# Up projection of a gated MLP: the sums of weight quarters made by VectorE in place of GpSimd

## The chip, the cores and the metric

The kernel runs on one core of one Trainium2 chip. The metric is the device time of one launch in microseconds, and several runs are given by their median. The engines are named as in the profile: PE is TensorE, DVE is VectorE, ACT is ScalarE, POOL is GpSimd, SP is SyncE, whose queue issues most of the transfers.

## The reference, cut to what matters

One layer of an encoder: a Fourier mixer, then a gated MLP with a centred convolution over positions. The change lies in the MLP's first matrix product.

```
D_MODEL = 1024; SEQ = 1024; D_FF = 2816; CONV_WIDTH = 3      # float32

def conv_gated_ffn(h, w_up, conv_w, conv_b, w_down):
    u = h @ w_up                                             # (1024, 1024) @ (1024, 5632)
    up = jnp.pad(u, ((0, 0), (1, 1), (0, 0)))
    u = up[:, :-2] * conv_w[0] + up[:, 1:-1] * conv_w[1] + up[:, 2:] * conv_w[2] + conv_b
    val, gate = u[..., :D_FF], u[..., D_FF:]
    return (jax.nn.gelu(gate, approximate=False) * val) @ w_down

# in the layer:
    h = modulate(x, sh2, sc2)
    y = conv_gated_ffn(h, ...)
    x = layer_norm(ALPHA * x + g2 * y, ...)
```

## The kernel before, in words

**Precision.** Every large product is made of three matmuls of a reduced-precision type: an operand is split into a high half (a copy by ScalarE, line 52) and a low half (source minus high half, by VectorE, line 53), and `hl3` (lines 292 to 294) adds high x high, high x low and low x high. A matmul that uses a weight's low half is the third of each three, line 294.

**Up projection.** The 2,816 columns of value and of gate are cut in 22 blocks of 128 each (`j`, 0 to 21). Blocks 0 and 1 are computed plainly (`first_mm`). From block 2 on, each block is one step of a scheme with seven products in place of eight: the two raw weight tiles of a block (`wu`, 512 KB each, loaded by `up_load`) hold four quarters A11, A21 (first tile) and A12, A22 (second tile), each [128, 4, 128]. Lines 764 to 767 make four sums of them: S1 = A21 + A22, S2 = S1 - A11, S3 = A11 - A21, S4 = A12 - S2. S1 and S2 share the tile in slot 31, S3 and S4 that in slot 32, so the sums of the next block can be written only when the last readers in this block are done.

The seven weight operands of a block, in the order of the products 0 to 6, are A11, S2, A12, S1, S3, S4, A22. `a_split` splits each into a_0 to a_6. The right-hand operands are quarters of the modulated, transposed activations (`h2t`, halves `Hh` and `Hl`) and the combinations T1, T2, T3, T4 of them, made once, in block 2. A product is 12 matmuls of 128x512 (four chunks of the inner dimension by three), a block 84. The results are added up by ScalarE (`p`) and VectorE (`u`, `uv`, `ug`), then convolved (line 678 on ScalarE, 679 and 680 on VectorE), put through GELU (685), multiplied (688 to 690) and written to DRAM by a transfer that GpSimd issues (691).

**Block 2** also finishes the plain blocks 0 and 1, makes T1 and T2 (line 658), adds to quarters in place with eight accumulating transfers that GpSimd issues (line 739), and splits T1 to T4. It runs by an order that is written out by hand for PE, DVE and ACT (`manual_schedule`, the table `between`); GpSimd and SP, and all engines from block 3 on, are put in order by the framework's scheduler. `A_first` gives the buffers of a_n in blocks 2 to 4: a_4 of block 2 lies in slot 30, into which the second raw tile of block 3 is loaded later.

**Down projection.** Seven passes over the block products, with the same scheme; it reads the blocks back from DRAM.

Of the kernel before, what the change touches and what calls it, by code (L numbers as in the profile page):

```python
# [11 lines left out]
ALU = mybir.AluOpType  # L12
# [23 lines left out]
def encoder_layer(ctx: ExitStack, tc: tile.TileContext, I, out: bass.AP):  # L36
    nc = tc.nc
    act, dve, pool, pe, sp = nc.scalar, nc.vector, nc.gpsimd, nc.tensor, nc.sync
# [6 lines left out]
    def slot(i, shape, dt, name):  # L45
        return big.tile([128] + list(shape), dt, tag=f"s{i}", name=name)
# [4 lines left out]
    def split(hi, lo, src, eng=None):  # L51
        act.activation(hi, src, AF.Copy)  # L52
        (eng or dve).tensor_tensor(lo, src, hi, ALU.subtract)  # L53

    def E(name):
        return pool if name in ON_POOL else dve
# [37 lines left out]
    def bank(i, name, shape=(512,)):  # L94
        return ps.tile([128] + list(shape), F32, tag=f"b{i}", name=name)
# [3 lines left out]
    def xbank(name):  # L99
        n_x[0] += 1  # L100
        return bank(n_x[0] % 8, name)
# [189 lines left out]
    def hl3(ps_ap, hi_l, lo_l, hi_r, lo_r, first, last):  # L291
        pe.matmul(ps_ap, hi_l, hi_r, start=first, stop=False)  # L292
        pe.matmul(ps_ap, hi_l, lo_r, start=False, stop=False)  # L293
        pe.matmul(ps_ap, lo_l, hi_r, start=False, stop=last)  # L294
# [252 lines left out]
    def up_load(j):  # L547
        sl = {0: (24, 27), 1: (40, 41), 3: (0, 30)}.get(j, (27, 30) if j % 2 else (28, 29))
        raws[j] = []
        for q in range(2):  # L550
            r = slot(sl[q], [4, 256], F32, f"wu{j}_{q}")
            sp.dma_start(r, I["w_up"][j, q])
            raws[j].append(r)
# [87 lines left out]
    def t_op(name, n, pieces):  # L641
        hi, lo = [], []
        for i in range(2):
            h = slot(T_slots[16 + 4 * n + 2 * i], [2, 512], F32R, f"T{name}h{i}")
            l = slot(T_slots[17 + 4 * n + 2 * i], [2, 512], F32R, f"T{name}l{i}")
            for q in range(2):
                split(h[:, q, :], l[:, q, :], pieces[2 * i + q])
                hi.append(h[:, q, :])
                lo.append(l[:, q, :])
        ops[name] = (hi, lo)  # L650

    def comb(name, x, y, op, sl):
        out_ = []
        for i in range(2):
            v = slot(sl + i, [2, 512], F32, f"{name}_{i}") if sl is not None else None
            for q in range(2):
                o = x[2 * i + q] if v is None else v[:, q, :]
                E(name).tensor_tensor(o, x[2 * i + q], y[2 * i + q], op)
                out_.append(o)
        return out_  # L660
# [4 lines left out]
    def plain_mm(acc, w, v, g):  # L665
        for k in range(KT):
            hl3(acc, *w[k, v], g(Hh[k]), g(Hl[k]), k == 0, k == KT - 1)

    def gated(j, u_v, u_g):
        gate_out(j, u_g, gate_conv(j, u_v, u_g))  # L670

    def gate_conv(j, u_v, u_g, tts=None, vs=(0, 1)):
        tv = []
        for v in vs:
            u = (u_v, u_g)[v]
            tt = slot(tts[v] if tts else 3 + (2 * j + v) % 3, [S], F32, f"t{j}_{v}")
            w = cw[:, j, v, :]
            act.activation(tt, u, AF.Identity, scale=w[:, 1:2], bias=w[:, 3:4])  # L678
            dve.scalar_tensor_tensor(tt[:, 1:S], u[:, 0 : S - 1], w[:, 0:1], tt[:, 1:S], ALU.mult, ALU.add)  # L679
            dve.scalar_tensor_tensor(tt[:, 0 : S - 1], u[:, 1:S], w[:, 2:3], tt[:, 0 : S - 1], ALU.mult, ALU.add)  # L680
            tv.append(tt)
        return tv

    def gate_out(j, u_g, tv):
        act.activation(tv[1], tv[1], AF.Gelu)
        gg = u_g

        dve.scalar_tensor_tensor(gg[:, 0:512], tv[0][:, 0:512], -1.0, tv[1][:, 0:512], ALU.mult, ALU.mult)
        dve.tensor_tensor(gg[:, 512:513], tv[0][:, 512:513], tv[1][:, 512:513], ALU.mult)
        dve.tensor_tensor(gg[:, 513:1024][:, ::-1], tv[0][:, 513:1024], tv[1][:, 513:1024], ALU.mult)  # L690
        pool.dma_start(gd[j], gg)  # L691
# [6 lines left out]
    def first_mm(j, gi):  # L698
        g = GRP[gi]
        for v in range(2):  # L700
            dst = g(uf[j][v])
            acc = bank((4, 5, 0, 1, 3)[n_f1[0] % 5], f"x{j}_{gi}{v}", tuple(dst.shape[1:]))
            n_f1[0] += 1
            plain_mm(acc, first_w[j], v, g)
            act.activation(dst, acc, AF.Copy)
# [23 lines left out]
    def t3_split(qs):  # L729
        for q in qs:  # L730
            split(ops["T3"][0][q], ops["T3"][1][q], B[0, 1][q])

    def minus(x):
        for v in x:
            act.activation(v, v, AF.Copy, scale=-1.0)

    def add_to(x, y):
        for q in range(4):
            pool.dma_start(x[q], y[q], accum_op=ALU.add)
# [4 lines left out]
        1: (lambda: t3_split(range(4)), lambda: tt.extend(gate_conv(0, *uf[0], tts=(34, 4), vs=(1,)))),  # L744
        2: (None, lambda: t_op("T4", 2, T2)),
        3: (None, lambda: gate_out(0, uf[0][1], tt)),
# [9 lines left out]
    for j in range(2, NB):  # L756
        up_load(j)
        raw = raws[j]
        A11, A21 = raw[0][:, :, 0:128], raw[0][:, :, 128:256]
        A12, A22 = raw[1][:, :, 0:128], raw[1][:, :, 128:256]  # L760
        S12 = slot(31, [2, 4, 128], F32, f"S12_{j}")
        S34 = slot(32, [2, 4, 128], F32, f"S34_{j}")
        S1, S2, S3, S4 = S12[:, 0], S12[:, 1], S34[:, 0], S34[:, 1]
        pool.tensor_tensor(S1, A21, A22, ALU.add)  # L764
        pool.tensor_tensor(S2, S1, A11, ALU.subtract)
        pool.tensor_tensor(S3, A11, A21, ALU.subtract)  # L766
        pool.tensor_tensor(S4, A12, S2, ALU.subtract)  # L767

        a_of = (A11, S2, A12, S1, S3, S4, A22)
        o_of = []  # L770

        def a_split(upto):
            while len(o_of) < min(upto, 7):
                n = len(o_of)
                o = slot(A_first.get(j, A_slots)[n], [2, 4, 128], F32R, f"a{j}_{n}")
                split(o[:, 0], o[:, 1], a_of[n])
                o_of.append(o)

        def product(n, tname):
            a_split(n + 1)  # L780
            acc = xbank(f"x{j}_{n}")
            th, tl = ops[tname]
            for kt in range(4):
                hl3(acc, o_of[n][:, 0, kt, :], o_of[n][:, 1, kt, :], th[kt], tl[kt], kt == 0, kt == 3)
            if j == 2:
                first, then = between[n]
                if first:
                    first()
                a_split(n + 4)
                if then:  # L790
                    then()
            return acc

        if j == 2:

            T1 = comb("T1", B[0, 1], B[0, 0], ALU.subtract, 25)
            minus(B[0, 1])
            add_to(B[0, 1], B[1, 1])
            T2 = comb("T2", B[1, 1], T1, ALU.subtract, 46)
            t_op("T2", 1, T2)  # L800
            minus(B[1, 0])
            add_to(T2, B[1, 0])
            a_split(1)
            first_mm(0, 3)
            tt = gate_conv(0, *uf[0], tts=(34, 4), vs=(0,))
            a_split(3)
            first_mm(1, 3)
        if j == NB - 1:
            g2 = slot(29, [D], F32, "g2")
            row_bcast(G2, g2, xbank)  # L810
        p12 = slot(6, [2, 512], F32, f"p12_{j}")
        u34 = slot(7, [2, 512], F32, f"u34_{j}")
        p1, u2, u3, u4 = p12[:, 0], p12[:, 1], u34[:, 0], u34[:, 1]
        uv_ = slot((2 * j) % 3, [S], F32, f"uv{j}")
        ug_ = slot((2 * j + 1) % 3, [S], F32, f"ug{j}")
        x = product(0, "B11")
        act.activation(p1, x, AF.Copy)
        x = product(1, "T2")
        dve.tensor_tensor(u2, x, p1, ALU.add)
        x = product(2, "B21")  # L820
        dve.tensor_tensor(uv_[:, 0:512], x, p1, ALU.add)
        x5 = product(3, "T1")
        dve.tensor_tensor(u4, x5, u2, ALU.add)
        x = product(4, "T3")
        dve.tensor_tensor(u3, x, u2, ALU.add)
        dve.tensor_tensor(ug_[:, 512:], x5, u3, ALU.add)
        x = product(5, "B22")
        dve.tensor_tensor(uv_[:, 512:], x, u4, ALU.add)
        x = product(6, "T4")
        dve.tensor_tensor(ug_[:, 0:512], u3, x, ALU.subtract)  # L830
        if j == 2:
            front.close()
        gated(j, uv_, ug_)
# [423 lines left out]
```

## Time and profile before

| | |
|---|---|
| median of 3 runs | 838.65 us (838.61 to 841.0) |
| the profiled execution | 838.94 us |
| its span, first to last instruction | 837.0 us |
| mean granted clock of TensorE | 0.987 of full speed |
| PE busy | 791.4 us (95%) |
| DVE busy | 691.4 us (83%) |
| ACT busy | 399.3 us (48%) |
| POOL busy | 253.5 us (30%) |

Times within a trace are microseconds from the span's start. In a timeline a row is a start, a duration and the instruction; a bracket at its end is the time for which the engine sat idle before it, and what released it. Durations of instructions that follow each other overlap by some 0.07 us on DVE and 0.16 us on PE, so the step from start to start is what a further instruction adds. The up projection by blocks of seven products runs from 218 to 608 us, the down projection behind it.

### The profile page before, as it was taken

To read this page: it belongs to the slowest core of one execution; us is meant where nothing else is said; L and a number is where in the kernel's file an instruction comes from. 1 tells how busy PE (TensorE), PEld (TensorE's weight loads), DVE (VectorE), ACT (ScalarE), POOL (GpSimd) and SP (SyncE) were. 2 spreads that over 40 slices of the span, in tenths; PEclk is the share of its full clock that TensorE was granted. 3 is DMA by queue.
4 is the path that set the end of the run, shared out by engine and by line. 5 is a ranking of instruction groups with operands and counts; after the bars stand their busy time and mean duration, and the time that the engine had idled before them with its cause. 6 is when DMAs were issued, how large, how long until landed. Compare 5 with 4: busy or idle time off the path is not lost.

```text
span 837.0 us, 10967 instructions
## 1 busy us (share of the span) xinstructions
PE 791.4 (95%) x4039; PEld 644.0 (77%) x4039; DVE 691.4 (83%) x1002; ACT 399.3 (48%) x605; POOL 253.5 (30%) x214
## 2 busy tenths in 40 slices
PE   2899999999989999999999999999999999999991
PEld 1566677899868888888888888888888878887881
DVE  6958866865899999998888888888688794557997
ACT  7643625785654534444444444344454425335611
POOL 2163004321743353343433333331000112602303
PEclk9999999999999999999999999999999999999996
DMA  9977864533731413222222222210498897998903
GB/s 340 376 261 251 277 225 170 201 114 141 138 113 51 151 53 114 102 86 76 76 79 98 94 83 90 88 51 25 152 369 324 257 327 141 190 163 213 302 14 126
DMA packets 51702, 136.01 MB, mean 162 GB/s; under 512 B 5672, under 2 KB 6824, under 8 KB 51648
## 3 DMA queue, kind: packets, MB, share of 16 engines
q1 hardware_dynamic: 39872, 105.16, 35.5%
q0 software_dynamic: 11776, 30.15, 15.2%
q8 instruction: 31, 0.51, 0.2%
q14 instruction: 23, 0.19, 0.1%
HBM read 110.39 MB, written 19.92 MB: 156 GB/s over the span
## 4 chain that ended last, share of the span: by engine, by line
PE 78%; DVE 11%; DMA 4%; ACT 3%; issue 3%; POOL 1%; POOLq 0%; SPq 0%; DVEq 0%; ACTq 0%
PE x L294 16%; PE x L292 16%; PE x L293 16%; PE o L293 7%; PE o L294 7%; PE o L292 7%; PE ada L139 2%; DMA gA<-gd 1%; DMA aw<-in_ada_w_dram 1%; DMA xr<-in_xm_dram 1%; DVE t L679 1%; DVE wa L366 1%; DVE we L366 1%; PE trm L530 1%; DVE sta L234 1%
## 5 line engine op out<-in xcount | busy, mean ns | idle before, releaser
L292 PE MATMUL x<-Hh,a 128*128 128x512 f32 (+2 forms) x448 | 161.7, 361 | 1.4 <-ACT a L52 1.4
L293 PE MATMUL x<-Hl,a 128*128 128x512 f32 (+2 forms) x448 | 161.0, 359 | 0.9 <-DVE Hl L53 0.9
L294 PE MATMUL x<-Hh,a 128*128 128x512 f32 (+2 forms) x448 | 160.9, 359 | 0.6 <-DVE a L53 0.6
L293 PE MATMUL o<-d_1l,d_0h 128*128 128x512 f32 (+1 forms) x299 | 113.8, 382 | 0.4 <-DVE d_1l L53 0.4
L294 PE MATMUL o<-d_1h,d_0l 128*128 128x512 f32 (+1 forms) x299 | 113.1, 381 | 0.0
L292 PE MATMUL o<-d_1h,d_0h 128*128 128x512 f32 (+1 forms) x299 | 102.1, 382 | 0.6 <-ACT d_0h L52 0.6
L52 ACT ACTIVATE a<-S 128x512 fp32r<-128x512 f32 x80 | 49.5, 628 | 101.6 <-PE x L294 75.6
L292 PEld LDWEIGHTS x<-Hh,a 128*128 128x128 f32 x448 | 84.6, 189 | 14.5 <-ACT a L52 1.8
L294 PEld LDWEIGHTS x<-Hh,a 128*128 128x128 f32 x448 | 84.5, 189 | 13.7 <-DVE a L53 1.1
L293 PEld LDWEIGHTS x<-Hl,a 128*128 128x128 f32 x448 | 84.5, 189 | 13.6 <-DVE Hl L53 1.1
L53 DVE TENSOR_TENSOR a<-S,a 128x512 fp32r<-128x512 f32 x80 | 65.2, 816 | 0.7
L292 PEld LDWEIGHTS o<-d_1h,d_0h 128*128 128x128 f32 x299 | 56.0, 188 | 12.0 <-ACT d_0h L52 1.0
L293 PEld LDWEIGHTS o<-d_1l,d_0h 128*128 128x128 f32 x299 | 56.1, 188 | 11.9 <-DVE d_1l L53 1.1
L294 PEld LDWEIGHTS o<-d_1h,d_0l 128*128 128x128 f32 x299 | 56.2, 188 | 10.7
L691 POOL DMA_DIRECT2D gd<-ug x20 | 11.5, 573 | 170.0 <-DVE ug L690 170.0
L53 DVE TENSOR_TENSOR a<-wu,a 128x512 fp32r<-128x512 f32 x60 | 53.5, 892 | 1.3 <-ACT a L52 1.1
L52 ACT ACTIVATE a<-wu 128x512 fp32r<-128x512 f32 x60 | 37.3, 625 | 19.0 <-PE x L294 12.1
L53 DVE TENSOR_TENSOR d_1l<-wd,d_1h 128x1024 fp32r<-128x1024 f32 (+1 forms) x37 | 43.9, 1190 | 2.8 <-ACT d_1h L52 2.7
L766 POOL TENSOR_TENSOR S<-wu 128x512 f32<-128x512 f32 x20 | 28.5, 1426 | 53.9 <-DVE a L53 53.9
L767 POOL TENSOR_TENSOR S<-wu,S 128x512 f32<-128x512 f32 x20 | 44.7, 2235 | 0.1
L679 DVE SCALAR_TENSOR_TENSOR t<-uv,cw,t 128x1023 f32<-128x1023 f32 x20 | 34.3, 1715 | 10.6 <-ACT t L678 10.6
L764 POOL TENSOR_TENSOR S<-wu,wu 128x512 f32<-128x512 f32 x20 | 32.1, 1603 | 34.7 <-DVE a L53 30.0
(316 smaller groups left out, 1837.9 us busy)
## 6 DMA issues: line engine op xcount, KB each, us to landing
aw<-in_ada_w_dram SPq DMA_DIRECT2D x48, 512.0 KB, 5.8
wu<-in_w_up_dram SPq DMA_DIRECT2D x44, 512.0 KB, 3.2
gd<-ug POOLq DMA_DIRECT2D x20, 512.0 KB, 2.9
wd<-in_w_down_dram SPq DMA_DIRECT2D x20, 512.0 KB, 11.6
gr<-gd SPq DMA_DIRECT2D x15, 512.0 KB, 6.6
gA<-gd SPq DMA_DIRECT2D x10, 512.0 KB, 13.1
Sg<-gd POOLq DMA_DIRECT2D x10, 512.0 KB, 7.8
x<-in_x_dram SPq DMA_DIRECT2D x8, 512.0 KB, 5.8
```

Of the source, the lines that this page charges most:

```text
L52: act.activation(hi, src, AF.Copy)
L53: (eng or dve).tensor_tensor(lo, src, hi, ALU.subtract)
L139: pe.matmul(pm[32 * g : 32 * g + 32, :], cb[:, kt, :], ws[kt][:, q * g : q * g + q], start=(kt == 0), stop=(kt == KT - 1), tile_position=( ...
L292: pe.matmul(ps_ap, hi_l, hi_r, start=first, stop=False)
L293: pe.matmul(ps_ap, hi_l, lo_r, start=False, stop=False)
L294: pe.matmul(ps_ap, lo_l, hi_r, start=False, stop=last)
L366: dve.tensor_tensor(w, w, g1, ALU.mult)
L679: dve.scalar_tensor_tensor(tt[:, 1:S], u[:, 0 : S - 1], w[:, 0:1], tt[:, 1:S], ALU.mult, ALU.add)
L691: pool.dma_start(gd[j], gg)
L764: pool.tensor_tensor(S1, A21, A22, ALU.add)
L766: pool.tensor_tensor(S3, A11, A21, ALU.subtract)
L767: pool.tensor_tensor(S4, A12, S2, ALU.subtract)
```

## The change

The four sums of a block are made by VectorE (`dve`) in place of GpSimd (`pool`), by the same operations on the same tiles. From block 3 on they stand where they stood in the program, ahead of the block's splits. In block 2, whose order on VectorE is written out by hand, S1 and S2 stand behind T2 and ahead of T2's split, and S3 and S4 behind the splits of a_0 to a_2.

```diff
-        pool.tensor_tensor(S1, A21, A22, ALU.add)
-        pool.tensor_tensor(S2, S1, A11, ALU.subtract)
-        pool.tensor_tensor(S3, A11, A21, ALU.subtract)
-        pool.tensor_tensor(S4, A12, S2, ALU.subtract)
+
+        def sums12():
+            dve.tensor_tensor(S1, A21, A22, ALU.add)
+            dve.tensor_tensor(S2, S1, A11, ALU.subtract)
+
+        def sums34():
+            dve.tensor_tensor(S3, A11, A21, ALU.subtract)
+            dve.tensor_tensor(S4, A12, S2, ALU.subtract)
+
+        if j > 2:
+            sums12()
+            sums34()
...
             T2 = comb("T2", B[1, 1], T1, ALU.subtract, 46)
+            sums12()
             t_op("T2", 1, T2)
...
             a_split(3)
+            sums34()
             first_mm(1, 3)
```

VectorE before, in block 2, from the last piece of T2 to the split of a_3 (`T_1` is the second half of T1 or T2, `TT2l` and `TT1l` are the low halves of T2 and T1, `S_2` the sums of block 2, `t_0` the convolution):

```order
L658 TENSOR_TENSOR T_1_2296<-h2t_1350,T_1_2282 128x512
L53 TENSOR_TENSOR TT2l_2300<-T_0_2293,TT2h_2299 128x512 x2
L53 TENSOR_TENSOR TT2l_2306<-T_1_2296,TT2h_2305 128x512 x2
L53 TENSOR_TENSOR a_0_2319<-wu_0_2269,a_0_2319 128x512
L679 SCALAR_TENSOR_TENSOR t_0_2374<-u_0_1743,cw,t_0_2374 128x1023
L680 SCALAR_TENSOR_TENSOR t_0_2374<-u_0_1743,cw,t_0_2374 128x1023
L53 TENSOR_TENSOR a_1_2378<-S_2_2273,a_1_2378 128x512
L53 TENSOR_TENSOR a_2_2381<-wu_1_2271,a_2_2381 128x512
L53 TENSOR_TENSOR TT1l_2454<-T_0_2279,TT1h_2453 128x512 x2
```

The same stretch of VectorE now:

```order
L658 TENSOR_TENSOR T_1_2292<-h2t_1350,T_1_2278 128x512
L766 TENSOR_TENSOR S_2_2273<-wu_0_2269,wu_1_2271 128x512
L767 TENSOR_TENSOR S_2_2273<-S_2_2273,wu_0_2269 128x512
L53 TENSOR_TENSOR TT2l_2298<-T_0_2289,TT2h_2297 128x512 x2
L53 TENSOR_TENSOR TT2l_2304<-T_1_2292,TT2h_2303 128x512 x2
L53 TENSOR_TENSOR a_0_2317<-wu_0_2269,a_0_2317 128x512
L679 SCALAR_TENSOR_TENSOR t_0_2372<-u_0_1743,cw,t_0_2372 128x1023
L680 SCALAR_TENSOR_TENSOR t_0_2372<-u_0_1743,cw,t_0_2372 128x1023
L53 TENSOR_TENSOR a_1_2376<-S_2_2273,a_1_2376 128x512
L53 TENSOR_TENSOR a_2_2379<-wu_1_2271,a_2_2379 128x512
L770 TENSOR_TENSOR S_2_2274<-wu_0_2269 128x512
L771 TENSOR_TENSOR S_2_2274<-wu_1_2271,S_2_2273 128x512
```

Four rows of sums have come in, two ahead of the split of T2 and two behind a_2; nothing else has changed place there.

GpSimd before, in block 2, from its first accumulating transfer to the sums of block 3 (`DMA` rows are transfers that it issues):

```order
L739 DMA h2t_1343<-h2t_1347 128x512
L764 TENSOR_TENSOR S_2_2273<-wu_0_2269,wu_1_2271 128x512
L739 DMA h2t_1344<-h2t_1348 128x512
L739 DMA h2t_1345<-h2t_1349 128x512
L739 DMA h2t_1346<-h2t_1350 128x512
L766 TENSOR_TENSOR S_2_2274<-wu_0_2269 128x512
L765 TENSOR_TENSOR S_2_2273<-S_2_2273,wu_0_2269 128x512
L739 DMA T_0_2293<-h2t_1347 128x512
L739 DMA T_0_2293<-h2t_1348 128x512
L739 DMA T_1_2296<-h2t_1349 128x512
L739 DMA T_1_2296<-h2t_1350 128x512
L767 TENSOR_TENSOR S_2_2274<-wu_1_2271,S_2_2273 128x512
```

GpSimd now, from the same transfer to the first two writes of finished blocks:

```order
L739 DMA h2t_1343<-h2t_1347 128x512
L739 DMA h2t_1344<-h2t_1348 128x512
L739 DMA h2t_1345<-h2t_1349 128x512
L739 DMA h2t_1346<-h2t_1350 128x512
L739 DMA T_0_2289<-h2t_1347 128x512
L739 DMA T_0_2289<-h2t_1348 128x512
L739 DMA T_1_2292<-h2t_1349 128x512
L739 DMA T_1_2292<-h2t_1350 128x512
L691 DMA gd<-u_1_1744 128x1024
L691 DMA gd<-u_1_1746 128x1024
```

The eight transfers follow each other, and behind them GpSimd issues the writes of blocks alone.

TensorE at the end of block 2, the same before and now (`x_5`, `x_6` are products 5 and 6 of block 2, `x_2` is product 2 of block 3):

```order
L294 MATMUL x_5_2568<-Hh_1636,a_5_2511 128x512
L292 MATMUL x_6_2586<-TT4h_2514,a_6_2540 128x512
L293 MATMUL x_6_2586<-TT4l_2515,a_6_2540 128x512
L292 MATMUL x_2_2671<-Hh_1633,a_2_2668 128x512
L293 MATMUL x_2_2671<-Hl_1641,a_2_2668 128x512
L294 MATMUL x_6_2586<-TT4h_2514,a_6_2540 128x512
```

Two matmuls of block 3 stand inside product 6. From there on the products of blocks 3 to 6 stand in another order than before; from block 7 on the products 0 to 6 follow each other in both.

## Rows read from the trace of the kernel before

**Rows 1.** The page's totals: busy us, share of the span, instructions of each engine.

```profile
PE 791.4 (95%) x4039; PEld 644.0 (77%) x4039; DVE 691.4 (83%) x1002; ACT 399.3 (48%) x605; POOL 253.5 (30%) x214
```

**Rows 2.** Waits of PE from 195 to 640 us: total us, times, longest.

```profile
PE x L294 <- DVE a L53: 3.6, 3, 1.8
PE x L292 <- ACT a L52: 1.4, 1, 1.4
```

**Rows 3.** Timeline of PE: start, us, instruction, idle time before it and releaser.

```profile
217.69 0.40 PE L292 MATMUL x<-Hh,a 128*128 128x512 f32 x1
...
222.87 0.50 PE L294 MATMUL x<-TT2h,a 128*128 128x512 f32 x1 [1.82 <-DVE a L53]
...
234.70 0.50 PE L294 MATMUL x<-Hh,a 128*128 128x512 f32 x1 [0.64 <-DVE a L53]
...
239.14 0.50 PE L292 MATMUL x<-Hh,a 128*128 128x512 f32 x1 [1.38 <-ACT a L52]
...
240.99 0.51 PE L294 MATMUL x<-TT4h,a 128*128 128x512 f32 x1 [1.12 <-DVE a L53]
...
248.65 0.39 PE L294 MATMUL x<-TT1h,a 128*128 128x512 f32 x1
...
608.16 0.39 PE L292 MATMUL o<-d_1h,d_0h 128*128 128x512 f32 x1
```

**Rows 4.** Timeline of DVE, one steady block (block 10 to 11).

```profile
391.72 0.69 DVE L825 TENSOR_TENSOR u<-x,p 128x512 f32<-128x512 f32 x1 [1.36 <-PE x L294]
392.44 1.26 DVE L53 TENSOR_TENSOR a<-S,a 128x512 fp32r<-128x512 f32 x1
...
396.45 1.86 DVE L679 SCALAR_TENSOR_TENSOR t<-uv,cw,t 128x1023 f32<-128x1023 f32 x1 [0.59 <-ACT t L678]
...
398.82 1.18 DVE L53 TENSOR_TENSOR a<-wu,a 128x512 fp32r<-128x512 f32 x1
...
401.13 1.27 DVE L679 SCALAR_TENSOR_TENSOR t<-ug,cw,t 128x1023 f32<-128x1023 f32 x1
...
410.76 0.69 DVE L825 TENSOR_TENSOR u<-x,p 128x512 f32<-128x512 f32 x1 [1.36 <-PE x L294]
```

**Rows 5.** Stretches: us; PE, PEld, DVE, ACT, POOL busy; PEclk, DMA share, GB/s.

```profile
238.00:243.00 5.00, 2.74 (x9) 1.88 (x9) 5.00 (x8) 2.47 (x5) 2.79 (x3) 0.89 0.19 57
243.00:250.00 7.00, 7.00 (x27) 5.68 (x26) 7.00 (x8) 1.66 (x3) 3.35 (x3) 0.83 0.47 177
...
310.00:320.00 10.00, 10.00 (x46) 8.29 (x45) 10.00 (x13) 5.02 (x9) 2.15 (x1) 1.00 0.30 105
```

**Rows 6.** Timeline of DVE in block 2.

```profile
207.43 2.49 DVE L658 TENSOR_TENSOR T<-h2t,T 128x512 f32<-128x512 f32 x4
209.83 2.49 DVE L53 TENSOR_TENSOR TT2l<-T,TT2h 128x512 fp32r<-128x512 f32 x4
...
215.14 4.61 DVE L679 SCALAR_TENSOR_TENSOR t<-u,cw,t 128x1023 f32<-128x1023 f32 x1 [0.98 <-ACT t L678]
219.79 2.43 DVE L680 SCALAR_TENSOR_TENSOR t<-u,cw,t 128x1023 f32<-128x1023 f32 x1
...
234.56 4.69 DVE L53 TENSOR_TENSOR TT4l<-T,TT4h 128x512 fp32r<-128x512 f32 x4
```

**Rows 7.** Timeline of POOL, in block 2 and in a steady block.

```profile
215.14 2.28 POOL L766 TENSOR_TENSOR S<-wu 128x512 f32<-128x512 f32 x1
...
217.62 4.54 POOL L739 DMA_DIRECT2D T<-h2t  x4
219.85 4.09 POOL L767 TENSOR_TENSOR S<-wu,S 128x512 f32<-128x512 f32 x1
...
397.18 2.28 POOL L767 TENSOR_TENSOR S<-wu,S 128x512 f32<-128x512 f32 x1
```

**Rows 8.** The page's DMA issues: KB each, median us from issue to landing.

```profile
wu<-in_w_up_dram SPq DMA_DIRECT2D x44, 512.0 KB, 3.2
```

**Rows 9.** The page's groups: a weight's high half on ACT (mean ns of one).

```profile
L52 ACT ACTIVATE a<-wu 128x512 fp32r<-128x512 f32 x60 | 37.3, 625 | 19.0 <-PE x L294 12.1
```

## The prediction

> **What bounds the kernel now.** I read the totals by engine first. TensorE is busy 95% of the span and VectorE 83%, GpSimd 30% [rows 1]. Two engines that full may each be the limit somewhere, so the next view is the list of what TensorE waits for between 195 and 640 us, which holds the up projection: only four waits, all on operand halves made by VectorE or ScalarE, 5.0 us together [rows 2]. TensorE's own instructions in order of time say where they lie and what they cost in all [rows 3]. Block 2 starts at 217.69 us. In the order of the program the row at 248.65 us is the 103rd of the up projection's 128x512 matmuls from there. A block has 84 such matmuls and the steady blocks repeat every 410.76 - 391.72 = 19.04 us [rows 4], which is 0.2267 us for each; 102 of them should take 23.12 us and took 30.96. So **7.84 us are lost in block 2**. The four waits make 4.96 of it. Most of the rest is the clock: right behind the last wait the granted clock is 0.89 and then 0.83 of full speed [rows 5], where TensorE had been idle four times since 220 us, and each restart costs about 0.1 us. From 248.65 to 608.16 us nothing more is lost: 1,578 matmuls at 0.2267 us are 357.7 us of the 359.5, and the remainder is about what eight small matmuls that spread a gate over the partitions need.
>
> So the up projection behind block 2 goes at TensorE's pace, and VectorE's time there is cover. How much of it is left, the busy time by stretch shows: VectorE is full until 320 us (10.00 of 10) [rows 5], and in the steady blocks it waits 1.36 and 0.59 us of 19.04 [rows 4], a tenth. A change that loads VectorE is paid for only if it eats that tenth; one that shortens VectorE's chain in block 2 can win up to 7.84 us.
>
> **What the change adds.** Four 128x512 additions or subtractions from SBUF per block, on VectorE. Four of this very kind take 2.49 us as a group with a step of 2.40 us to the next group [rows 6], so 0.60 us each and 2.40 us a block. Blocks 2 to 21 are 20 blocks: 48 us of VectorE.
>
> **What it removes.** GpSimd's sums, and with them what they cost VectorE. In the steady block three VectorE instructions run long exactly while GpSimd has a sum in hand: a low half of 1.26 us and one of 1.18 us where an instruction of this size takes 0.69, and a convolution step of 1.86 us where its twin takes 1.27 [rows 4]; GpSimd's last sum of the block, 397.18 to 399.46 us, lies over the last two [rows 7]. That gives back 0.57 + 0.49 + 0.59 = 1.65 us. VectorE's steady block was 19.04 less two waits of 1.36 and 0.59 us, so 17.09 us; the waits are the only idle time of that block, and it becomes 17.09 + 2.40 - 1.65 = **17.84 us of 19.04**. It still fits, with 1.2 us to spare, so the steady blocks should not move.
>
> The Trainium skill ("SBUF — State Buffer", section "Who interferes with whom") says that a VectorE instruction with two SBUF inputs contends with a GpSimd instruction that reads SBUF, and that the one that comes second blocks wholly until the first is done. The trace agrees in direction and not in size: the last sum holds GpSimd for 2.28 us and the two rows beside it are long by 1.08 us together. By whole blocks that sum alone would give back 2.28, and VectorE's block would end near 16.6 us.
>
> **Block 2, where the gain is.** Here GpSimd's sums hit harder. The first convolution step takes 4.61 us from 215.14 us in place of 1.27, the second 2.43; four low halves of T4 take 4.69 us where four such took 2.49 [rows 6]. GpSimd's S3 and S4 of that block start at 215.14 and 219.85 us, in the places of the first two [rows 7]; the third lies where it makes the sums of block 3. That is 3.34 + 1.16 + 2.20 = 6.7 us of VectorE's chain, against 2.4 us that the block's four sums add to it.
>
> I then lay the new order out with those steps (0.60 us each 128x512 instruction, 1.20 us each convolution step, which is the step behind a row of 1.27). T1 and T2 are ready at 209.83 us [rows 6]; S1 and S2 follow to 211.0, the low halves of T2 to 213.4, a_0 to 214.1. The convolution waits for ScalarE as before and starts at 215.14; its two steps end at 217.5, and the low half of a_1 at 218.1. TensorE wants that at 217.69 + 14 x 0.2267 = 220.9 us: the first wait (1.82 us) is gone with 2.8 us to spare. On: a_2 218.8, S3 and S4 220.0, low halves of T1 222.4, a_3 223.0, low halves of T3 225.4, a_4 226.0, two convolution steps 228.4, one sum from PSUM 229.0, a_5 229.6, low halves of T4 232.0, one sum 232.6, a_6 233.2, up to 0.5 us later with the handovers from ScalarE. Without a wait TensorE starts product 5 at 217.69 + 60 x 0.2267 = 231.3 us and product 6 at 234.0; it wants the low half of a_5 at 231.7 and that of a_6 at 234.9, behind two matmuls of the next block. Both are there, a_5 by 1.6 and a_6 by 1.2 us at best. So the waits of 0.64 and 1.12 us go too.
>
> The wait of 1.38 us goes only in part. It is for a_2 of block 3, whose raw quarter lands in the buffer that block 2's a_4 leaves free. Its load can start when product 4 is over, at 231.4 us in the new time, takes 3.2 us to land [rows 8] and needs a ScalarE copy of 0.62 us [rows 9]: 235.3 us. TensorE wants it at 217.69 + 74 x 0.2267 = 234.5, so **0.8 us of waiting stays**, 1.0 with the restart. With one short wait in place of four I take the clock to stay at its upper level of 2.4 GHz: it fell only behind the last of the four [rows 3, 5].
>
> Block 3 and 4: VectorE has the next sums and the backlog in its queue; going on by the same steps its low halves of block 3 are ready at 238.0 (a_2), 242.2 (a_3) and 245.8 (a_1), against 238.3, 243.5 and 249.0 us at which TensorE would reach them; in block 4 it is about 5 us ahead. The tightest is a_2, with 0.3 us.
>
> **The sum.** 7.84 - 1.0 = 6.8 us gained in block 2, nothing in the rest of the up projection. Behind it TensorE goes straight on into the down projection and its loads start when up-projection buffers come free, so the 6.8 us should reach the end. The profiled execution took 838.94 us, so 832.1; the median of the runs shown, 838.65, is 0.3 lower. I say **832.0 us**. The bounds: if the 0.8 us vanish too (a faster load), 831.0, with the 0.3 us 830.7; if TensorE's wait for a_2 becomes 2 us and the clock falls as before (7.84 - 4.96 - 0.4 = 2.5 us), 838.94 - 7.84 + 4.5 = 835.6.
>
> **Rivals.**
> *The load decides.* The quarter for a_2 of block 3 comes later than 235.3 us, since its queue also carries block 4's loads ahead of it. For: the load waits for TensorE and cannot start earlier. Against: 3.2 us is the median of 44 [rows 8]. At twice that, 3.2 us more are lost: 835.3, and with the clock's 2.5 us 837.8.
> *The descriptors, not the sums, slow VectorE.* From 217.62 us GpSimd also issues four accumulating transfers [rows 7], which stay. If those made the long rows, the convolution keeps about 3 us of its 4.6 + 2.4, a_1 arrives near 221.5 and a_6 near 237: half of the loss stays and the time is about 835.5. Against it: the steady block has no such transfers at 392 to 400 us and its rows are long all the same.
> *Slower.* VectorE is full from 238 to 320 us, and the change puts 2.4 us a block on it. If the long rows were VectorE's own and nothing came back, its steady block would be 17.09 + 2.40 = 19.49 us and longer than TensorE's 19.04: 0.45 us a block over some 17 blocks, and 2 x 2.4 us in blocks 2 and 3, so 838.94 + 7.7 + 4.8 = 851. It decides from a give-back under 0.45 us a block; the rows show 1.65. The Trainium skill ("Perfetto Trace Analysis", section "Optimizing Scalar/DVE Operations") would move work off a saturated VectorE, GpSimd included, but adds that this might not help between these two as they share a read port. The first half speaks for this rival; the trace has the long rows that the second half leads one to expect.
> *Nothing.* The sums don't bind and other waits fill block 2: within 0.3% of 838.65 (836.1 to 841.2; a measurement of this kernel cannot tell less from no change).
>
> **Chances.** Forecast (830.5 to 834) 0.62; the load 0.12 and the descriptors 0.10, of which most ends below 836.1; nothing 0.08; slower 0.08. So faster 0.81, same 0.11, slower 0.08. The range for 8 in 10 goes from 830.5 to 836.5: the forecast and most of the two middle rivals, less the rest.
>
> **What would show it.** Right: between 217 and 250 us one wait of TensorE under 1.5 us, on ScalarE's a; a granted clock of 1.00 throughout; the convolution step near 215 us at 1.3 us; VectorE's rows at 0.69 and 1.27 in the steady block, its waits together near 1.2 us a block, GpSimd busy near nothing from 250 to 590. Wrong: waits of TensorE on VectorE in blocks 3 to 6, VectorE without any idle time in the steady blocks, or a long convolution row beside the transfers alone.

## The result

The changed kernel takes **832.11 us** (median of 6 runs, 831.44 to 833.74) against 838.63 us before, a ratio of 0.9916 (95% interval 0.9905 to 0.9927). 832.0 was forecast. The profiled execution took 831.87 us with a span of 830.1 us.

The totals answer to [rows 1] (busy us, share of the span, instructions), on the page of the changed kernel:

```profile
PE 789.0 (95%) x4039; PEld 642.8 (77%) x4039; DVE 694.5 (84%) x1082; ACT 400.2 (48%) x605; POOL 122.2 (15%) x134
```

VectorE has 80 instructions more and is busy only 3.1 us longer; GpSimd's busy time is halved. Taken alone this says nothing on the gain. The waits of TensorE between 195 and 640 us (total, times, longest) do; there is one in place of the four of [rows 2]:

```profile
PE x L292 <- ACT a L52: 0.7, 1, 0.7
```

TensorE's timeline has the same places as [rows 3]: the start of block 2, the wait, the start of the down projection.

```profile
217.38 0.40 PE L292 MATMUL x<-Hh,a 128*128 128x512 f32 x1
...
235.07 0.50 PE L292 MATMUL x<-Hh,a 128*128 128x512 f32 x1 [0.73 <-ACT a L52]
...
601.28 0.39 PE L292 MATMUL o<-d_1h,d_0h 128*128 128x512 f32 x1
```

Blocks 2 to 21 take 601.28 - 217.38 = 383.90 us, where they took 390.47: **6.57 us**, all in block 2. The 103rd matmul of block 2 and 3 comes 24.30 us after the first, where the pace alone needs 23.12, so 1.18 us of the 7.84 are left. Behind 601.28 us the span goes on for 228.82 us, before for 228.84; the rest of the difference between the two profiled executions is 0.31 us of earlier entry into block 2 and 0.2 us outside the span.

The stretches of [rows 5] (us; PE, PEld, DVE, ACT, POOL busy; granted clock; DMA share, GB/s) show the clock at its upper level where its mean had been 0.89 and 0.83:

```profile
238.00:243.00 5.00, 5.00 (x23) 4.00 (x22) 5.00 (x8) 2.42 (x4) 0.00 (x0) 1.00 0.32 110
243.00:250.00 7.00, 7.00 (x32) 5.79 (x31) 7.00 (x11) 3.26 (x4) 0.00 (x0) 1.00 0.00 0
```

VectorE in block 2, to be laid beside [rows 6]:

```profile
210.84 2.49 DVE L53 TENSOR_TENSOR TT2l<-T,TT2h 128x512 fp32r<-128x512 f32 x4
...
214.84 1.28 DVE L679 SCALAR_TENSOR_TENSOR t<-u,cw,t 128x1023 f32<-128x1023 f32 x1 [0.90 <-ACT t L678]
216.15 1.28 DVE L680 SCALAR_TENSOR_TENSOR t<-u,cw,t 128x1023 f32<-128x1023 f32 x1
...
229.74 2.49 DVE L53 TENSOR_TENSOR TT4l<-T,TT4h 128x512 fp32r<-128x512 f32 x4
```

All three long rows are gone. In the same microseconds GpSimd still issues the transfers that [rows 7] showed from 217.62 us:

```profile
212.06 3.56 POOL L739 DMA_DIRECT2D T<-h2t  x4 [1.04 <-ACT h2t L735]
```

They lie over the end of TT2l and the start of the convolution step at 214.84 us, and both go at their usual pace. The transfers were not what slowed VectorE.

For the steady blocks one timeline row shows little; the table of VectorE's groups by form over 250 to 590 us shows all of it (line, engine, operation, tiles, shape, count | busy us, mean ns of one | idle before). Before:

```profile
L53 DVE TENSOR_TENSOR a<-S,a 128x512 fp32r<-128x512 f32 x74 | 61.1, 827 | 0.7
L53 DVE TENSOR_TENSOR a<-wu,a 128x512 fp32r<-128x512 f32 x55 | 48.7, 887 | 0.0
L679 DVE SCALAR_TENSOR_TENSOR t<-uv,cw,t 128x1023 f32<-128x1023 f32 x19 | 33.0, 1738 | 9.3 <-ACT t L678 9.3
...
L825 DVE TENSOR_TENSOR u<-x,p 128x512 f32<-128x512 f32 x18 | 12.4, 687 | 15.0 <-PE x L294 15.0
```

After:

```profile
L53 DVE TENSOR_TENSOR a<-S,a 128x512 fp32r<-128x512 f32 x72 | 49.2, 685 | 0.3 <-ACT a L52 0.3
L53 DVE TENSOR_TENSOR a<-wu,a 128x512 fp32r<-128x512 f32 x54 | 36.8, 682 | 0.3 <-ACT a L52 0.2
L679 DVE SCALAR_TENSOR_TENSOR t<-uv,cw,t 128x1023 f32<-128x1023 f32 x19 | 24.2, 1276 | 0.7 <-ACT t L678 0.7
...
L835 DVE TENSOR_TENSOR u<-x,p 128x512 f32<-128x512 f32 x18 | 12.3, 684 | 3.1 <-PE x L294 3.1
```

The instructions with two operands in SBUF were long in the mean and are not any more: 74 x 0.142 + 55 x 0.205 + 19 x 0.462 = 30.6 us over the 17.9 blocks of the stretch, and with the other convolution steps and the last products of the plain blocks about 34, so 1.9 us a block in the mean of this stretch, whose first blocks stand in another order than the steady ones. The instruction that reads `x` from PSUM (line 825, now 835) was at 687 ns beside GpSimd's sums already and is at 684 now.

### The profile page after: what moved, and what is told of

Its sections match the earlier page's. It is cut to its first block, busy times and chain, and to the rows that moved or that the text cites. A ratio compares the mean times of both kernels' runs of the same rounds, so it can differ in the third digit from the quotient of the medians.

```text
span 830.1 us, 10891 instructions
## 1 busy us (share of the span) xinstructions
PE 789.0 (95%) x4039; PEld 642.8 (77%) x4039; DVE 694.5 (84%) x1082; ACT 400.2 (48%) x605; POOL 122.2 (15%) x134
## 4 chain that ended last, share of the span: by engine, by line
PE 81%; DVE 10%; DMA 4%; issue 2%; ACT 1%; POOL 1%; POOLq 0%; SPq 0%; DVEq 0%; ACTq 0%
PE x L292 17%; PE x L294 17%; PE x L293 17%; PE o L293 7%; PE o L294 7%; PE o L292 7%; PE ada L139 2%; DMA gA<-gd 1%; DMA wu<-in_w_up_dram 1%; DMA aw<-in_ada_w_dram 1%; DMA xr<-in_xm_dram 1%; DVE wa L366 1%; DVE we L366 1%; PE trm L530 1%; DVE sta L234 1%
## 5 line engine op out<-in xcount | busy, mean ns | idle before, releaser
L53 DVE TENSOR_TENSOR a<-S,a 128x512 fp32r<-128x512 f32 x80 | 54.7, 685 | 0.3 <-ACT a L52 0.3
L52 ACT ACTIVATE d_0h<-Sg 128x1024 fp32r<-128x1024 f32 x15 | 15.9, 1062 | 53.2 <-PE o L293 53.2
L53 DVE TENSOR_TENSOR a<-wu,a 128x512 fp32r<-128x512 f32 x60 | 40.9, 682 | 0.4 <-ACT a L52 0.2
L52 ACT ACTIVATE d_1h<-wd 128x1024 fp32r<-128x1024 f32 (+1 forms) x37 | 37.7, 1022 | 6.1 <-DMA wd<-in_w_down_dram 3.5
L53 DVE TENSOR_TENSOR d_0l<-Sg,d_0h 128x1024 fp32r<-128x1024 f32 x15 | 18.4, 1223 | 23.9 <-ACT d_0h L52 23.9
L292 PE MATMUL x<-TT2h,a 128*128 128x512 f32 x80 | 31.2, 390 | 0.0
```

## The experiments

Times of runs are medians; "blocks" is the time from the first matmul of block 2 to the first of the down projection, from the profiled execution (390.47 us before, 383.90 after).

### Each part alone

Block 2 alone by VectorE:

```diff
         if j > 2:
-            sums12()
-            sums34()
+            pool.tensor_tensor(S1, A21, A22, ALU.add)
+            pool.tensor_tensor(S2, S1, A11, ALU.subtract)
+            pool.tensor_tensor(S3, A11, A21, ALU.subtract)
+            pool.tensor_tensor(S4, A12, S2, ALU.subtract)
```

> Only block 2 makes its four sums on VectorE; blocks 3 to 21 leave them on GpSimd, as before the change. If the gain is block 2's chain on VectorE alone, nearly all of it is here: the first two waits of TensorE (1.82 and 0.64 us) are gone, the convolution steps near 215 us take 1.3 us, and only the four low halves of T4 stay long (about 4.7 us), since the sums of block 3 still lie beside them; a_6 then comes 1 to 2 us later than in the changed kernel. Time 832 to 834, TensorE full from 250 us on. If the steady blocks carry the gain, this run stays near 838.

833.48 us against 839.41, ratio 0.9929 (0.9914 to 0.9945), blocks 385.33 us. VectorE, with the step near 215 us and T4's split:

```profile
213.66 1.28 DVE L679 SCALAR_TENSOR_TENSOR t<-u,cw,t 128x1023 f32<-128x1023 f32 x1 [0.90 <-ACT t L678]
...
228.57 3.60 DVE L53 TENSOR_TENSOR TT4l<-T,TT4h 128x512 fp32r<-128x512 f32 x4
```

GpSimd, with the first sum of block 3, which it makes again:

```profile
228.74 1.67 POOL L776 TENSOR_TENSOR S<-wu 128x512 f32<-128x512 f32 x1 [14.29 <-DVE a L53]
```

Most of the gain comes back with block 2's own sums. T4's split is too long by 1.11 us, exactly where GpSimd has one sum in hand; 4.7 us had been expected for it, as before, where two sums lay beside it.

The rest alone, as an edit of the kernel before: block 2's sums by GpSimd, those from block 3 on by VectorE.

```diff
-        pool.tensor_tensor(S1, A21, A22, ALU.add)
-        pool.tensor_tensor(S2, S1, A11, ALU.subtract)
-        pool.tensor_tensor(S3, A11, A21, ALU.subtract)
-        pool.tensor_tensor(S4, A12, S2, ALU.subtract)
+        eng = pool if j == 2 else dve
+        eng.tensor_tensor(S1, A21, A22, ALU.add)
+        eng.tensor_tensor(S2, S1, A11, ALU.subtract)
+        eng.tensor_tensor(S3, A11, A21, ALU.subtract)
+        eng.tensor_tensor(S4, A12, S2, ALU.subtract)
```

> The reverse: block 2's sums stay on GpSimd, blocks 3 to 21 make theirs on VectorE. By the theory of block 2's chain the first wait of 1.8 us and the convolution steps of 4.6 and 2.4 us are still there, the low halves of T4 shrink to 2.5 us, and a_6 comes some 2 us earlier: 1.3 to 2.9 us gained, 835.7 to 837.3. If the change were worth something in the steady blocks, this run would be near 832.

836.73 us, ratio 0.9969 (0.9956 to 0.9983), blocks 388.42 us. VectorE:

```profile
214.57 4.61 DVE L679 SCALAR_TENSOR_TENSOR t<-u,cw,t 128x1023 f32<-128x1023 f32 x1 [0.98 <-ACT t L678]
219.22 2.44 DVE L680 SCALAR_TENSOR_TENSOR t<-u,cw,t 128x1023 f32<-128x1023 f32 x1
...
233.98 2.49 DVE L53 TENSOR_TENSOR TT4l<-T,TT4h 128x512 fp32r<-128x512 f32 x4
```

The two long steps are back to within 0.01 us of [rows 6], and T4's split is short: it was block 3's sums that stretched it. So the long rows divide between the two parts as the prediction had them: 3.34 and 1.16 us by block 2's sums, 2.20 us by those of block 3. The gains of the parts by blocks are 5.14 and 2.05 us, together 0.6 more than the whole. The granted clock stayed at 1.00 in either run, so the 1.6 us that its drop cost before (below, "The clock") stand in both gains. They are most of the second: its four waits still come to 4.4 us against 4.96, so VectorE's shorter chain alone won some 0.5. No part of the gain of the second comes from the steady blocks, in which TensorE waits neither before nor after.

### Do GpSimd's sums slow VectorE, or what else stands there?

To the changed kernel (with a_4 of block 2 in slot 5, next section) four additions by GpSimd were added that nobody reads, in the place where its sums had stood:

```diff
+            idle, u01 = slot(30, [2, 512], F32, "idle"), uf[0][1]
+            for k in range(4):
+                pool.tensor_tensor(idle[:, k % 2], u01[:, 384:896], u01[:, 130:642], ALU.add)
```

> The kernel of the run before it (a_4 in buffer 5), and GpSimd makes four additions of 128x512 in block 2 that nobody reads, from where the columns of block 0 are complete (about 213.7 us), behind its eight accumulating transfers. VectorE's, ScalarE's and TensorE's instructions stand in the same order. If GpSimd's work beside it is what made VectorE slow, the instructions of VectorE between 215 and 225 us grow again, by 2 to 5 us together, and waits of TensorE on VectorE come back: 833 to 837. If it was the lateness of GpSimd's results, or the transfers, the time is that of the run before it within 0.5 us.

834.9 us, ratio 0.996 (0.9947 to 0.9973), blocks 387.88 us, 3.94 more than without them. VectorE:

```profile
214.19 3.00 DVE L679 SCALAR_TENSOR_TENSOR t<-u,cw,t 128x1023 f32<-128x1023 f32 x1 [0.90 <-ACT t L678]
217.22 2.00 DVE L680 SCALAR_TENSOR_TENSOR t<-u,cw,t 128x1023 f32<-128x1023 f32 x1
219.14 1.58 DVE L53 TENSOR_TENSOR a<-S,a 128x512 fp32r<-128x512 f32 x1
220.64 1.57 DVE L53 TENSOR_TENSOR a<-wu,a 128x512 fp32r<-128x512 f32 x1
222.13 0.68 DVE L770 TENSOR_TENSOR S<-wu 128x512 f32<-128x512 f32 x1
```

GpSimd:

```profile
213.79 2.30 POOL L816 TENSOR_TENSOR idle<-u 128x512 f32<-128x512 f32 x1
214.85 3.26 POOL L816 TENSOR_TENSOR idle<-u 128x512 f32<-128x512 f32 x1
216.17 3.97 POOL L816 TENSOR_TENSOR idle<-u 128x512 f32<-128x512 f32 x1
218.19 3.45 POOL L816 TENSOR_TENSOR idle<-u 128x512 f32<-128x512 f32 x1
```

The four VectorE instructions inside the additions are long by 4.2 us together, the one behind them is not. From 210 to 225 us VectorE has no listed wait for GpSimd, and nothing reads what the additions make: what is left is the access to SBUF. This undoes 3.94 of some 6.5 us without undoing the change.

The same place with writes in place of additions: one addition of 8 columns, then 16 writes of a constant, read by nothing.

```diff
+            pool.tensor_tensor(idle[:, 0, 0:8], u01[:, 400:408], u01[:, 500:508], ALU.add)
+            for k in range(16):
+                pool.memset(idle[:, 0], 0.0)
```

> The kernel of the slot run (a_4 of block 2 in another buffer) with one GpSimd addition of 8 columns and then 16 GpSimd writes of a constant to 128x512, none of them read by anything, in the place where the idle additions stood in the run before (some 8 us of GpSimd from 213.8 us). The idle additions lengthened VectorE's chain by 4.2 us and cost 1.9 us. If it is GpSimd's reading of SBUF that holds VectorE, which the Trainium skill (SBUF page, section on who interferes with whom) has as the condition, writes alone do nothing: VectorE's convolution steps near 215 us at 1.3 us each, and 832.5 to 833.5. If any GpSimd access holds it, the steps are 2 to 3 us and the time is 834.5 to 836.

829.68 us, ratio 0.9891 (0.9876 to 0.9906), blocks 383.27 us. GpSimd, then VectorE:

```profile
214.37 9.29 POOL L817 MEMSET idle<- 128x512 f32 x16
```

```profile
214.31 1.28 DVE L680 SCALAR_TENSOR_TENSOR t<-u,cw,t 128x1023 f32<-128x1023 f32 x1
215.51 0.69 DVE L53 TENSOR_TENSOR a<-S,a 128x512 fp32r<-128x512 f32 x1
...
218.15 2.49 DVE L53 TENSOR_TENSOR TT1l<-T,TT1h 128x512 fp32r<-128x512 f32 x4
```

9.29 us of GpSimd writes lie over VectorE instructions with two SBUF operands, and not one is long. It is GpSimd's reading that costs. The total, however, was lower than any theory had said, by some 3 us; the next section is on that.

Half and half: S1 and S2 by VectorE, S3 and S4 by GpSimd, in all blocks.

```diff
-            dve.tensor_tensor(S3, A11, A21, ALU.subtract)
-            dve.tensor_tensor(S4, A12, S2, ALU.subtract)
+            pool.tensor_tensor(S3, A11, A21, ALU.subtract)
+            pool.tensor_tensor(S4, A12, S2, ALU.subtract)
```

> S1 and S2 on VectorE, S3 and S4 on GpSimd, in all blocks. If each GpSimd sum lengthens the VectorE instructions beside it, two of the four still do: in block 2 the step near 215 us or a low half next to S3 or S4 stays long, some 1 to 3 us of the 6.7 us; the time lies between 833 and 836, with steady VectorE between 17.1 and 17.9 us a block. If only S1's long run (5.15 us) did harm, the time is that of the changed kernel, 832 to 833.

834.01 us, ratio 0.9937 (0.9922 to 0.9952), blocks 602.86 - 216.82 = 386.04 us. VectorE's S2 and T2's split fell beside the two GpSimd sums:

```profile
209.68 2.66 DVE L767 TENSOR_TENSOR S<-S,wu 128x512 f32<-128x512 f32 x1
212.26 3.58 DVE L53 TENSOR_TENSOR TT2l<-T,TT2h 128x512 fp32r<-128x512 f32 x4
```

```profile
209.12 2.66 POOL L770 TENSOR_TENSOR S<-wu 128x512 f32<-128x512 f32 x1
212.42 1.67 POOL L771 TENSOR_TENSOR S<-wu,S 128x512 f32<-128x512 f32 x1 [0.64 <-DVE S L767]
```

Half the sums, half the stretching (2.0 and 1.1 us in block 2): not S1 alone, the other sums do it too to the two-operand instruction that stands beside them.

### The wait that stayed

The one wait left is for a load into the buffer of a_4 of block 2. With that a_4 in another slot the load can start earlier:

```diff
-    A_first = {2: [45, 44, 48, 45, 30, 48, 45], ...
+    A_first = {2: [45, 44, 48, 45, 5, 48, 45], ...
```

> The changed kernel, with the operand a_4 of block 2 in buffer 5 in place of buffer 30, so that the second raw weight tile of block 3 can be loaded some 6 us earlier. The scheduler then puts two matmuls each of products 1, 2 and 3 of block 3 inside product 6 of block 2. If the one wait that is left (0.73 us, for that tile's load) hangs on the load, it goes; the same place then waits for ScalarE's copies a_1, a_2, a_3, up to 0.5 us in all. Time 831.2 to 832.2. If something else than the load holds that place, the time and the wait stay as in the changed kernel.

832.97 us, ratio 0.9923 (0.991 to 0.9937), blocks 383.94 us: nothing. The waits of TensorE in the up projection:

```profile
PE x L294 <- DVE a L53: 0.6, 1, 0.6
```

The wait on ScalarE is gone, and one on VectorE has taken its place: with the quarter there early, the scheduler put S1 and S2 of block 3 into VectorE's chain ahead of and inside T4's split, and a_6 came 1.0 us later.

In the kernel with the idle writes this went better by accident (the writes hold the slot until 223.7 us, the load comes later, and S1 of block 3 stands behind T4's split): one wait of 0.3 us. Was that worth its 829.68 us? The changed kernel, the idle writes again, and the idle writes' kernel with only its 8-column addition, together on one chip:

> The changed kernel once more, beside the kernel with the idle writes. The idle writes gave 829.7 us on a chip on which the changed kernel had not run. If that chip runs this kernel faster, the changed kernel gives about 830 where the idle writes do; if the idle writes' kernel is really faster, the changed kernel stays at 832 to 833.

> The kernel with the idle writes unchanged. Against the changed kernel it has a_4 of block 2 in another buffer, the load for block 3's second tile held back by the writes, and so S1 and S2 of block 3 behind T4's split on VectorE. Its profile showed one wait of 0.3 us in block 2 in place of 0.7, which explains 0.5 us; it also entered block 2 1.85 us earlier by an unchanged order, which nothing in it explains. If only the order counts: 831.5 to 832.5, 0.5 us under the changed kernel. If the earlier start is its own: 829 to 830.5.

> The kernel of the idle writes with the 16 writes left out, only the 8-column addition stays; on every engine its order is that of the slot run, so S1 of block 3 stands in the chain ahead of T4 again. If the writes do nothing but set the order: 832.5 to 833.5, as the slot run (832.97). If the buffer of a_4 is what gives the idle writes' kernel its time: 829.5 to 830.5.

831.61 us (blocks 384.05), 831.09 us (383.26) and 831.8 us (383.94) against 838.45 before; the ratios are 0.9918, 0.9914 and 0.9918, with intervals of some 0.0018 to either side. So the low time did not repeat; in its profile it comes from entering block 2 at 215.53 us, 1.85 us before the changed kernel's. In the thirteen profiles of this case that entry lies between 215.5 and 219.1 us, and the order of TensorE, VectorE and ScalarE up to there is the same in all of them but for the sums themselves; two profiles of one kernel differ in it by 1.7 us (215.53 and 217.26). The stage repeats far better, 383.90 and 384.05, 383.27 and 383.26, 383.94 and 383.94. By it the better order gains 0.7 us on the changed kernel; the total time can't show that.

### How much room is left on VectorE

S1 made twice, and four times, more per block from block 3 on (the same values again; the second kernel has 4 for the 2):

```diff
         if j > 2:
+            for _ in range(2):
+                dve.tensor_tensor(S1, A21, A22, ALU.add)
             sums12()
```

> The changed kernel with S1 made twice more per block from block 3 on, on VectorE (the same values again), 2 x 0.60 = 1.2 us a block. If the steady blocks go at TensorE's pace and VectorE has the idle time left that its busy share shows (46.27 of 50 us, so 17.62 of 19.04 a block), the block becomes 18.8 us and still fits: within 1.5 us of the changed kernel's 832.1, VectorE's busy share from 400 to 450 us near 0.99. If VectorE's time binds already, each block costs 1.2 us more, some 19 blocks: about 855.

> The changed kernel with S1 made four times more per block from block 3 on, on VectorE, 2.4 us a block: 17.62 + 2.40 = 20.0 us against TensorE's 19.04. If the room is the 1.4 us that the busy share shows, about 1.0 us a block is lost over some 18 blocks, less what VectorE is ahead at the start: 842 to 851, with waits of TensorE on VectorE in the steady blocks. This is also what the slower rival would have looked like had nothing been given back. If room remains from somewhere else (waits that are not needed), under 836.

Two more: 837.62 us (835.3 to 840.59), ratio 0.9989 (0.9973 to 1.0005), blocks 388.70 us. The forecast of at most 1.5 us more was wrong and the steady part of it right. Waits of TensorE, in its timeline, up to the last one:

```profile
246.77 0.51 PE L294 MATMUL x<-TT1h,a 128*128 128x512 f32 x1 [1.60 <-DVE a L53]
...
250.43 0.50 PE L292 MATMUL x<-Hh,a 128*128 128x512 f32 x1 [0.64 <-ACT a L52]
...
258.23 0.50 PE L292 MATMUL x<-Hh,a 128*128 128x512 f32 x1 [0.30 <-DVE p L831]
```

All lie before 260 us; later there is none. There VectorE still has the backlog of the plain blocks, and the added sums cost 4.80 us by blocks; in the steady blocks 1.2 us more a block cost nothing.

Four more: 850.93 us (846.96 to 853.0), ratio 1.0136 (1.0104 to 1.0167). A convolution step of successive blocks on VectorE:

```profile
449.62 1.34 DVE L679 SCALAR_TENSOR_TENSOR t<-uv,cw,t 128x1023 f32<-128x1023 f32 x1
...
468.87 1.35 DVE L679 SCALAR_TENSOR_TENSOR t<-uv,cw,t 128x1023 f32<-128x1023 f32 x1
```

The block is 19.25 us now, and VectorE sets it: from 400 to 556 us it has no idle time at all. Its work as steps from start to start is, in the changed kernel, 18 instructions of 0.60, four convolution steps of 1.20 and the three of the final product, 1.27: 16.87 us; with 2.40 added 19.27. So the room was 19.04 - 16.87 = **2.2 us a block**. The 0.2 us too much are only some 2.3 us of the 16.8 that the blocks lost, since TensorE's blocks follow every 19.04 us until 383 us and every 19.27 only then. Some 10 us lie in blocks 2 and 3, with a wait of 5.19 us ahead of 252.94 us and the clock behind it, and 4.1 in a wait before the down projection:

```profile
252.94 0.79 PE L292 MATMUL x<-TT1h,a 128*128 128x512 f32 x1 [5.19 <-ACT a L52]
...
619.81 0.80 PE L292 MATMUL o<-d_1h,d_0h 128*128 128x512 f32 x1 [4.15 <-ACT d_0h L52]
```

```profile
253.00:260.00 7.00, 5.84 (x12) 3.73 (x13) 7.00 (x10) 2.20 (x4) 0.00 (x0) 0.50 0.06 24
```

So 1.2 us a block on top of the change leave the steady blocks as they are, and 2.4 bring the mechanism of the rival "slower".

## Why the prediction was right, point by point

**The 7.84 us in block 2, as what can be won.** Right. 1.18 us are left of it, and the gain of the stage is 6.57 us against 6.8. That 832.0 and 832.11 lie so close is in part luck: the stage gave 0.2 us less than forecast and the rest of the profiled execution 0.5 us more, and the runs scatter by 2.3 us.

**The long rows are GpSimd's doing.** Right, and shown from both sides: they go with its sums (the whole change, and each part alone), come back with additions that have nothing to do with the kernel, and do not come with transfers or writes. With that the rival of the descriptors falls. The 6.7 us leave out a fourth row of before, the low half of a_2 beside S4, which is 0.85 us too long:

```profile
222.96 1.54 DVE L53 TENSOR_TENSOR a<-wu,a 128x512 fp32r<-128x512 f32 x1
```

**The order laid out by hand in block 2.** The lows of a_1, a_5 and a_6 were forecast at 218.1, 229.6 and 233.2 to 233.7 us, for an entry 0.31 us later than it was; they ended at 218.0, 229.8 and 233.4. Less the earlier entry, a_5 and a_6 are 0.5 us later than the bare sum and at the end of the half microsecond that had been left for handovers. The three waits on VectorE went.

**The wait that stays.** Forecast 0.8 us, 1.0 with the restart, on ScalarE's a; measured 0.73, and 0.1 at the restart. ScalarE's copy follows the load at once:

```profile
234.38 1.15 ACT L52 ACTIVATE a<-wu 128x512 fp32r<-128x512 f32 x2 [0.63 <-DMA wu<-in_w_up_dram]
```

**The clock.** It stayed at 1.00, its upper level of 2.4 GHz, as forecast. The 0.89 and 0.83 of [rows 5] are means over stretches that hold both levels; from 241.9 to 245.3 us the clock was at the lower one, 1.2 GHz:

```profile
241.90:245.30 3.40, 3.40 (x10) 2.63 (x9) 3.40 (x3) 1.45 (x3) 1.92 (x2) 0.50 0.83 305
```

Steps of TensorE were 0.43 us there in place of 0.227, 1.6 us of the 7.84. The run with the rest alone kept three waits on VectorE and one on ScalarE, 4.4 us in all, and showed 1.00 all the same. So the drop before was not the price of such a row of waits as such, and the 2.5 us of the pessimistic bound had less behind them than they seemed. The mean granted clock of the runs before lies between 0.985 and 0.991, so whether it fell in block 2 in each of them is open.

**VectorE's steady block, 17.84 us with 1.2 to spare.** Right in that it fits, mis-sized in its room. The term that failed is 17.09, the block less its two listed waits: at handovers some steps are 0.1 to 0.2 us longer than a bare one, which isn't listed as a wait and isn't work either. The give-back of 1.65 us holds for the steady block, and the sum of the steps leaves 2.2 us. With no give-back at all the steps would have come to 16.87 + 1.65 = 18.5 us, still under TensorE's 19.04: by them the steady part of the rival "slower" could not have happened, and its price there was too high.

**Whole instructions or parts.** By the Trainium skill ("SBUF — State Buffer", section "Who interferes with whom") a VectorE instruction with two SBUF inputs contends with GpSimd's reads and not with its writes, nor does one with a single SBUF input. All three are borne out: 827 and 887 ns against 685, 1.28 us beside the writes, 687 ns for the sums from PSUM. That the second comer blocks until the first is done, as the prediction has it from there, the runs show as well, in size too. The prediction took S4's 2.28 us for one whole block and found the rows too short for it; that was a misreading of [rows 4, 7], which leave out two sums of the same block:

```profile
391.86 1.29 POOL L765 TENSOR_TENSOR S<-S,wu 128x512 f32<-128x512 f32 x1
...
395.94 1.29 POOL L766 TENSOR_TENSOR S<-wu 128x512 f32<-128x512 f32 x1 [2.78 <-DVE a L53]
```

VectorE's low half of 392.44 us ends 0.55 us behind the end of S2, its convolution step of 396.45 us 1.08 us behind the end of S3, and its low half of 398.82 us 0.55 us behind the end of S4: each began with a sum in hand and did its own work behind it. S4 itself began beside the convolution step and ends 1.16 us behind it; with nothing in hand a sum takes 1.29 us, and the rest of the 2.28 is waiting. In the run with idle additions the two engines go strictly by turns. GpSimd's additions end at 216.09, 218.11, 220.14 and 221.64 us, VectorE's four instructions at 217.19, 219.22, 220.72 and 222.21 us, each but the first 0.6 to 1.1 us behind the end of the one before it on the other engine. So VectorE's four take 7.94 us (214.19 to 222.13) where they take 3.96 in the changed kernel (214.84 to 218.80 us), and GpSimd's 7.85 where four alone would take 5.2: from the first start to the last end 8.4 us, not far under the sum of the two, 9.1.

**Moving work on to a full engine.** The Trainium skill ("Perfetto Trace Analysis", section "Optimizing Scalar/DVE Operations") would take work from a full VectorE, to GpSimd among others, and adds that with these two it might not help. Here the addition decides: in block 2 GpSimd's sums, the block's own and two of block 3, cost VectorE more than 6.7 us, and making the four itself costs 2.4.

**To the end undiminished.** Right: 228.82 us behind the stage against 228.84.

**The load as a rival.** It came in time: TensorE waited 0.73 us for it. In the slot run, where it no longer binds, nothing was won, since VectorE's chain in that run's order is 0.6 us behind it.

## What to carry over

Before work is put on GpSimd to spare VectorE, or taken back, look at how long VectorE's two-operand SBUF instructions are beside it and away from it, by shape; the difference is part of the price, and it can be larger than the work that was moved. Read what such a row waited for from the ends of the other engine's rows: a long row can hold a wait of its own. Judge it in the stage where VectorE's chain is waited for, and measure the room elsewhere as the sum of the steps, not as the block less its listed waits. And compare the stage that a change touches from profile to profile: here it repeats to 0.15 us, while the changed kernel's total scatters by 2.3.

## What the runs showed of the hardware

VectorE's instructions with two operands in SBUF and GpSimd's additions from SBUF do not run side by side: the rows above end one behind the other. A GpSimd sum that gets in between two such instructions of a full VectorE costs it some 1.1 us here: 1.11 for the one in T4's split of the run with block 2 alone, 2.20 for the two before. Who gets in when both wait is another matter. Before, GpSimd's S1 took four times its 1.28 us while VectorE's additions and splits ran on one behind the other at their full pace [rows 6], and it ended when VectorE had been idle for 1.15 us:

```profile
208.32 5.15 POOL L764 TENSOR_TENSOR S<-wu,wu 128x512 f32<-128x512 f32 x1
```

```profile
213.47 0.69 DVE L53 TENSOR_TENSOR a<-wu,a 128x512 fp32r<-128x512 f32 x1 [1.15 <-ACT a L52]
```

From 215.14 us on it was VectorE's step that waited, through two sums [rows 6, 7]: it ends at 219.75 us, 1.09 us behind the second.

```profile
216.39 2.27 POOL L765 TENSOR_TENSOR S<-S,wu 128x512 f32<-128x512 f32 x1
```

No run here varied the order alone, so why GpSimd got no turn in the first case, two in the second and every other one with the idle additions stays open. So does the second step of [rows 6], 2.43 us from 219.79 us: S4, beside it, ends only at 223.94 us, so no sum's end accounts for it.

The granted clock fell to 0.50, the lower level of 1.2 GHz, behind a wait of 5.19 us (four more sums), fell to the same level behind four waits of 0.6 to 1.8 us before, and stayed at 1.00 behind four waits of 0.55 to 1.84 us in the run with the rest alone. What tells the last two apart is open too.
